# Decoder trunk: seven products in feed-forward blocks 3 and 5 too, quarter sums on GpSimd, and recorded draws for the order search

## The chip, the cores and the metric

The kernel runs on one core of one Trainium2 chip. The metric is the device time of one launch in microseconds (us); before the change it is 2908.55 us, the median of three runs (2907.97 to 2912.36). The engines are named as in the profile: PE is TensorE (matmul), DVE is VectorE, ACT is ScalarE, POOL is GpSimd, SP issues the DMAs.

## The reference, cut to what matters

The program is a decoder trunk of four layers over 512 tokens of 1024 features in float32. Each layer is a token mixer (sparse attention, mLSTM, RWKV-7, sparse attention again) followed by a gated feed-forward with a causal convolution of width 3, each after an RMSNorm and with a residual add. The change touches the feed-forward:

```
def conv_ffn(h, w_up, conv_w, conv_b, w_down):
    gate, val = jnp.split(h @ w_up, 2, axis=-1)
    gate = causal_dwconv(gate, conv_w, conv_b)
    return (jax.nn.silu(gate) * val) @ w_down
...
for i in range(DEPTH):
    h = rmsnorm(x, norm_mixer[i])
    x = x + mixer(h)
    h = rmsnorm(x, norm_ffn[i])
    x = x + conv_ffn(h, ffn_w_up[i], ffn_conv_w[i], ffn_conv_b[i], ffn_w_down[i])
return rmsnorm(x, final_norm)
```

The inner width is 2816, which is 22 blocks of 128 channels for the gate and 22 for the value.

## The kernel before, in words

**Layout.** The residual x is held feature-major, eight tiles of 128 features by 512 tokens. Every float32 product is made of three fp32r matmuls: each operand is split into a rounded part (hi, written by ACT) and the rest (lo, a subtraction on DVE, `split` at L741 and L742, and `weights` at L469 and L470), and hi·hi, lo·hi and hi·lo are summed in PSUM.

**A feed-forward stage** (`ffn`) goes over 22 blocks b. A block is made in one of two ways.

- *Plain* (`up`, `fm_block`, `mm3`): two outputs, gate and value, of 8 chunks with 3 matmuls of 512 columns each, 48 matmuls (L475 to L477). DVE makes two low weight parts of 128x1024 (L470) and the gate's scaling by R (L615).
- *Seven products* (`seven`): gate and value rows of the weight and the two halves of the contraction make a 2x2 arrangement, and so do contraction halves and token halves of the input. Seven products of 4 chunks with 3 matmuls of 256 columns give all four quarters of the result: 84 matmuls (L624). For it DVE makes four sums of weight quarters (`add`, L644), the low parts of seven weight tiles (`ring`, L742, tile slo) and seven combinations of PSUM results of 128x256 (L658 to L673).

Both end in the gate's two convolution steps on DVE (L593, L595), the product of value and gate (L602) and its split (alo). In the kernel before, SEVEN names blocks 2, 4 and 6 to 21, so that blocks 0, 1, 3 and 5 are plain.

**The input's combinations.** The seven products read four combined inputs besides plain quarters of x. `combos` makes them once in each stage: ACT scales the eight tiles of x (L549, tile tmp), then for each of four pairs four subtractions or additions of 128x256 (L558 to L561) give two tiles, and each is split into bhi (ACT) and blo (DVE, L742). The 16 operations of 128x256 stand on DVE.

**The norm beside it.** At a stage's start PE sums the squares by eight small matmuls with ones (L518, after the last of seven running sums on POOL, L509), DVE turns them into the reciprocal root rc by twelve small operations (L525, then `rsqrt`, L448 to L453), PE transposes rc (L534) and ACT copies it out as R. These transposes stand in PE's order among the matmuls of the first blocks, so what follows them on PE waits for rc.

**Down products.** `down_part` makes the partial output products of blocks 0 to 5 (from block 6 on) and of 6 to 13, one of eight outputs after each block; the rest comes at the end. They need the activations of those blocks.

**What sets the order.** The program is traced once, and class `Order` then chooses each engine's instruction order by list scheduling with durations of its own (`cost`, `LATENCY`). POOL and DVE are separate engines in it and nothing ties a POOL operation to a DVE operation beyond data. `best` searches: for each of eight phases (four mixers, four feed-forwards) 24 starting priorities with random spreads, ten rounds of `turns` each, the best few joined to what comes before, and at the end 13 perturbed passes over the whole program. Engines then run their instructions strictly in the chosen order.

Of the kernel before, what the change touches and what calls it, by code (L numbers as in the profile page):

```python
# [16 lines left out]
OP = mybir.AluOpType  # L17
# [3 lines left out]
T = 512  # L21
# [3 lines left out]
FB = 22  # L25
EPS = 1e-6

SEVEN = (2, 4) + tuple(range(6, FB))
PARTS = [6, 14]


# [16 lines left out]
TABLE = {"Silu": 1, "Sigmoid": 2, "Gelu_apprx_tanh": 3, "Exp": 0, "Tanh": 0}  # L48
SWITCH = 1283
AVOID = 500  # L50
SPREADS = (0, 50, 50, 50, 200, 200, 200, 500, 500, 500, 1000, 1000, 1000)
TICK, WARM = 10240 / 3, 3060.0
BESIDE = 22

# [1 line left out]
class Order:  # L56
# [290 lines left out]
                prio = [-(s + d) for s, d in zip(late, self.dur)]  # L347
        return best

    def best(self, tries=24, rounds=10, keep=4, log=None):  # L350

        rng = random.Random(1)
        prio, at = [], 0.0
        for a, b in zip(self.phases, self.phases[1:] + [len(self.ins)]):
            p, whole = self.part(a, b), self.part(0, b)
            found = []
            for i in range(tries):
                spread = (0, 300, 1000, 3000)[min(i, 1 + i % 3)]
                found.append(p.turns([100.0 * k + rng.gauss(0, spread) for k in range(b - a)], rounds, at))
            found.sort(key=lambda f: f[0])  # L360
            joined = []
            for T, start in found:
                t, end = whole.run(prio + [at + s for s in start])
                joined.append((end, t))
                if len(joined) == keep and max(joined)[0] - min(joined)[0] < 8000:
                    break
            end, start = min(joined, key=lambda f: f[0])
            if log:
                log(f"phase {a}-{b}: best {found[0][0]/1e3:.1f} mean {sum(f[0] for f in found)/len(found)/1e3:.1f} joined", *["%.1f" % ((e - at) / 1e3) for e, _ in joined])
            prio, at = start, end  # L370
        found = [(at, prio)] + [self.turns([s + rng.gauss(0, spread) for s in prio], 2) for spread in SPREADS]
        if log:
            log("whole:", *["%.1f" % (T / 1e3) for T, _ in found])
        return min(found, key=lambda f: f[0])

    def apply(self, tc, start):
        info = mybir.DependencyInfo(mybir.DependencyClass.NoSync, mybir.DependencyReason.DATA)
# [8 lines left out]
class Core:  # L386
# [153 lines left out]
    def combos(self, g, ap):  # L540


        nc, v = self.nc, self.nc.vector
        H = T // 2
        hx = {}

        def scaled(i):
            hx[i] = self.tmp()
            nc.scalar.activation(hx[i], self.x[i], AF.Copy, scale=g[:, i:i + 1])  # L549
            self.spill(i, self.x[i])  # L550

        out = []
        for k, need in enumerate(((0, 4, 1), (5, 2, 3), (6,), (7,))):
            for i in need:
                scaled(i)
            a, b = hx[k], hx[k + 4]
            t, u = self.tmp(), self.tmp()
            v.tensor_tensor(t[:, :H], a[:, :H], a[:, H:], op=OP.subtract)  # L558
            v.tensor_tensor(t[:, H:], b[:, H:], t[:, :H], op=OP.add)
            v.tensor_tensor(u[:, :H], a[:, H:], b[:, H:], op=OP.subtract)  # L560
            v.tensor_tensor(u[:, H:], b[:, :H], t[:, H:], op=OP.subtract)  # L561
            for w in (t, u):
                hi = self.xp.tile([128, T], F32R, name="bhi", tag="x", bufs=DC)
                lo = ap.tile([128, T], F32R, name="blo", tag="blo", bufs=DC)
                self.split(hi, lo, w)
                out.append((hi, lo))
        return out

    def ffn(self, ly, gcur, gnext, nsplit=True):
        nc, tc, A = self.nc, self.tc, self.A  # L570
        H = T // 2
        with ExitStack() as es:
# [132 lines left out]
            for b in range(FB):  # L705
# [5 lines left out]
                slots[b] = free.pop(0) if free else len(slots)  # L711
                block = (seven if b in SEVEN else plain_block)(b)
                next(block)
# [1474 lines left out]
```

## Time and profile before

| what | value |
|---|---|
| runs | 2907.97, 2908.55, 2912.36 us |
| the profiled execution's own time | 2905.92 us |
| its span in the profile | 2904.2 us, mean granted TensorE clock 0.982 |
| busy on PE, DVE, ACT, POOL | 96%, 81%, 56%, 28% of the span |
| four feed-forward stages | from 370, 963, 1838 and 2542 us, some 351 to 362 us each |

A row of a timeline gives start, duration, engine, source line, operation, and tiles written and read. Consecutive starts give the pitch, which on PE and DVE is below the duration, since an engine begins an instruction while the one before drains. A window row gives the busy time of each engine in a stretch, with the number of instructions in brackets.

### The profile page before, as it was taken

To read this page: it belongs to the slowest core of one execution; us is meant where nothing else is said; L and a number is where in the kernel's file an instruction comes from. 1 tells how busy PE (TensorE), PEld (TensorE's weight loads), DVE (VectorE), ACT (ScalarE), POOL (GpSimd) and SP (SyncE) were. 2 spreads that over 40 slices of the span, in tenths; PEclk is the share of its full clock that TensorE was granted. 3 is DMA by queue.
4 is the path that set the end of the run, shared out by engine and by line. 5 is a ranking of instruction groups with operands and counts; after the bars stand their busy time and mean duration, and the time that the engine had idled before them with its cause. 6 is when DMAs were issued, how large, how long until landed. Compare 5 with 4: busy or idle time off the path is not lost. (4 is left out here: it accounts for less than half of the span.)

```text
span 2904.2 us, 48935 instructions
## 1 busy us (share of the span) xinstructions
PE 2789.4 (96%) x17960; PEld 2357.7 (81%) x17960; DVE 2363.3 (81%) x4225; ACT 1622.5 (56%) x3290; POOL 820.8 (28%) x898
## 2 busy tenths in 40 slices
PE   7999999999989999998899999999998999999998
PEld 6777889998867899986666676899987877889996
DVE  8688789897697889979557874889978688699985
ACT  4677665544575555444446665655544677565543
POOL 5476300001063100013456653100004576300001
PEclk9999999999999999999989999999999999999999
DMA  4200133445213434453200012334453100233444
GB/s 163 66 29 24 66 109 112 136 137 188 87 46 110 131 104 130 135 178 111 75 35 3 9 30 73 118 104 130 140 158 139 59 30 23 79 99 125 137 129 145
DMA packets 115423, 283.30 MB, mean 98 GB/s; under 512 B 14448, under 2 KB 26224, under 8 KB 115184
## 3 DMA queue, kind: packets, MB, share of 16 engines
q1 hardware_dynamic: 115184, 280.18, 29.7%
q8 instruction: 142, 2.33, 0.3%
q14 instruction: 97, 0.79, 0.1%
HBM read 248.67 MB, written 31.46 MB: 96 GB/s over the span
## 5 line engine op out<-in xcount | busy, mean ns | idle before, releaser
L469 ACT ACTIVATE whi<-wraw 128x1024 fp32r<-128x1024 f32 (+2 forms) x344 | 272.2, 792 | 418.6 <-PE ps L477 273.8
L624 PE MATMUL ps<-h,shi 128*128 128x256 f32 x1728 | 352.1, 281 | 0.0
L470 DVE TENSOR_TENSOR wlo<-wraw,whi 128x512 fp32r<-128x512 f32 (+2 forms) x306 | 272.6, 892 | 72.2 <-ACT whi L469 70.5
L624 PE MATMUL ps<-bhi,slo 128*128 128x256 f32 x1152 | 322.3, 280 | 0.0
L624 PE MATMUL ps<-blo,shi 128*128 128x256 f32 x1152 | 322.0, 281 | 0.0
L624 PE MATMUL ps<-bhi,shi 128*128 128x256 f32 x1152 | 321.8, 281 | 0.0
L609 POOL MEMSET tmp<- 128x2 f32 x88 | 8.2, 99 | 1098.0 <-DVE tmp L602 875.3
L624 PEld LDWEIGHTS ps<-h,shi 128*128 128x128 f32 x1728 | 282.5, 188 | 6.7
L477 PE MATMUL ps<-alo,whi 128*128 128x512 f32 x704 | 278.0, 395 | 0.0
L475 PE MATMUL ps<-ahi,whi 128*128 128x512 f32 x704 | 277.6, 395 | 0.0
L476 PE MATMUL ps<-ahi,wlo 128*128 128x512 f32 x704 | 277.1, 394 | 0.0
L475 PE MATMUL ps<-h,whi 128*128 128x512 f32 x672 | 266.0, 398 | 4.0 <-ACT whi L469 1.2
L476 PE MATMUL ps<-h,wlo 128*128 128x512 f32 x672 | 264.1, 394 | 2.0 <-DVE wlo L470 1.7
L477 PE MATMUL ps<-h,whi 128*128 128x512 f32 x672 | 263.6, 394 | 0.0
L624 PE MATMUL ps<-h,slo 128*128 128x256 f32 x864 | 242.6, 281 | 0.0
L741 ACT ACTIVATE shi<-sum 128x512 fp32r<-128x512 f32 x288 | 179.6, 625 | 110.9 <-DVE sum L644 81.2
L742 DVE TENSOR_TENSOR slo<-sum,shi 128x512 fp32r<-128x512 f32 x288 | 197.9, 688 | 47.0 <-ACT shi L741 45.4
L624 PEld LDWEIGHTS ps<-bhi,slo 128*128 128x128 f32 x1152 | 217.0, 188 | 5.2
L624 PEld LDWEIGHTS ps<-bhi,shi 128*128 128x128 f32 x1152 | 216.5, 188 | 4.5
L624 PEld LDWEIGHTS ps<-blo,shi 128*128 128x128 f32 x1152 | 216.5, 188 | 1.2
L509 POOL TENSOR_TENSOR tmp<-tmp 128x512 f32<-128x512 f32 x62 | 96.6, 1557 | 352.4 <-ACT tmp L504 348.1
L1097 POOL TENSOR_SCALAR P<-P,st,GT 128x384 f32<-128x384 f32 (+3 forms) x256 | 161.8, 646 | 81.8 <-DVE st L1095 52.0
(669 smaller groups left out, 7745.9 us busy)
## 6 DMA issues: line engine op xcount, KB each, us to landing
wraw<-in_fup_dram SPq DMA_DIRECT2D x104, 512.0 KB, 3.7
fraw<-in_fup_dram SPq DMA_DIRECT2D x72, 512.0 KB, 3.5
wraw<-in_fdn_dram SPq DMA_DIRECT2D x128, 256.0 KB, 2.7
share<-xt SPq DMA_DIRECT2D x64, 256.0 KB, 2.2
xt<-share SPq DMA_DIRECT2D x64, 256.0 KB, 3.0
wraw<-in_fdn_dram SPq DMA_DIRECT2D x64, 192.0 KB, 2.6
x<-spill SPq DMA_DIRECT2D x48, 256.0 KB, 3.1
spill<-x SPq DMA_DIRECT2D x47, 256.0 KB, 2.7
```

Source lines behind the costliest of these rows:

```text
L469: nc.scalar.activation(hi[:, s], raw[:, s], AF.Copy)
L470: (nc.gpsimd if pool else nc.vector).tensor_tensor(lo[:, s], raw[:, s], hi[:, s].bitcast(F32), op=OP.subtract)
L475: t.matmul(ps, whi, xhi, start=start, stop=False)
L476: t.matmul(ps, wlo, xhi, start=False, stop=False)
L477: t.matmul(ps, whi, xlo, start=False, stop=stop)
L509: nc.gpsimd.tensor_tensor(a2, self.acc[0], sq, op=OP.add)
L609: nc.gpsimd.memset(G[:, 0:2], 0.0)
L624: nc.tensor.matmul(ps, lhs[:, s], x, start=start and k + i == 0, stop=k == 3 and i == 2, skip_group_check=True)
L741: self.nc.scalar.activation(hi, src, AF.Copy)
L742: self.nc.vector.tensor_tensor(lo, src if src2 is None else src2, hi.bitcast(F32), op=OP.subtract)
L1097: po.tensor_scalar(P[qb], P[qb], st[:, 2, qb:qb + 1], GT[:, qb, 3 * h + 1 + br:3 * h + 2 + br], op0=OP.mult, op1=OP.mult)
```

## The change

Three things change. SEVEN becomes blocks 2 to 21, so blocks 3 and 5 of each of the four stages are made by seven products too. The 16 operations of `combos` go from DVE to POOL. `best` no longer searches: it takes one recorded seed and spread for each phase and one perturbed pass at the end, which gives another order throughout the program, the mixers included.

```
-SEVEN = (2, 4) + tuple(range(6, FB))
+SEVEN = tuple(range(2, FB))
...
-SPREADS = (0, 50, 50, 50, 200, 200, 200, 500, 500, 500, 1000, 1000, 1000)
+DRAWS = ((21, 300), (13, 1000), (13, 1000), (10, 1000), (15, 300), (4, 1000), (3, 300), (11, 3000))
+LAST = (1008, 500)
...
-    def best(self, tries=24, rounds=10, keep=4, log=None):
+    def best(self):
...
-        for a, b in zip(self.phases, self.phases[1:] + [len(self.ins)]):
-            p, whole = self.part(a, b), self.part(0, b)
-            found = []
-            for i in range(tries):
-                spread = (0, 300, 1000, 3000)[min(i, 1 + i % 3)]
-                found.append(p.turns([100.0 * k + rng.gauss(0, spread) for k in range(b - a)], rounds, at))
...
-        found = [(at, prio)] + [self.turns([s + rng.gauss(0, spread) for s in prio], 2) for spread in SPREADS]
...
-        return min(found, key=lambda f: f[0])
+        for a, b, (seed, spread) in zip(self.phases, self.phases[1:] + [len(self.ins)], DRAWS):
+            rng = random.Random(seed)
+            t, start = self.part(a, b).turns([100.0 * k + rng.gauss(0, spread) for k in range(b - a)], 10, at)
+            prio, at = self.part(0, b).run(prio + [at + s for s in start])
+        if LAST is None:
+            return at, prio
+        rng = random.Random(LAST[0])
+        return self.turns([s + rng.gauss(0, LAST[1]) for s in prio], 2)
...
-            v.tensor_tensor(t[:, :H], a[:, :H], a[:, H:], op=OP.subtract)
-            v.tensor_tensor(t[:, H:], b[:, H:], t[:, :H], op=OP.add)
-            v.tensor_tensor(u[:, :H], a[:, H:], b[:, H:], op=OP.subtract)
-            v.tensor_tensor(u[:, H:], b[:, :H], t[:, H:], op=OP.subtract)
+            po.tensor_tensor(t[:, :H], a[:, :H], a[:, H:], op=OP.subtract)
+            po.tensor_tensor(t[:, H:], b[:, H:], t[:, :H], op=OP.add)
+            po.tensor_tensor(u[:, :H], a[:, H:], b[:, H:], op=OP.subtract)
+            po.tensor_tensor(u[:, H:], b[:, :H], t[:, H:], op=OP.subtract)
```

Line numbers of the changed kernel from `combos` on are 12 below those of the kernel before (L742 becomes L730).

How the order moves is shown at three places. First, DVE at the start of the first feed-forward stage, before: x, gains, h are the residual's split, ms, rq_t, rc and rq_u the norm's small tiles, tmp the combinations, blo their low parts.

```order
L497 SCALAR_TENSOR_TENSOR h_4157<-x_85,gains_88,h_4156 128x512
L644 TENSOR_TENSOR sum_4437<-fraw_4431 128x512
L558 TENSOR_TENSOR tmp_4275<-tmp_4263 128x256
L560 TENSOR_TENSOR tmp_4276<-tmp_4263,tmp_4267 128x256
L559 TENSOR_TENSOR tmp_4275<-tmp_4267,tmp_4275 128x256
L525 TENSOR_SCALAR ms_4240<-ps_4235 128x4
L561 TENSOR_TENSOR tmp_4276<-tmp_4267,tmp_4275 128x256
L448 TENSOR_SCALAR rq_t_4243<-ms_4240 128x4
L558 TENSOR_TENSOR tmp_4301<-tmp_4271 128x256
L449 TENSOR_SCALAR rc_4242<-rq_t_4243 128x4
L560 TENSOR_TENSOR tmp_4302<-tmp_4271,tmp_4289 128x256
L451 TENSOR_TENSOR rq_u_4244<-rc_4242 128x4
```

The same place now, on DVE:

```order
L485 SCALAR_TENSOR_TENSOR h_4157<-x_85,gains_88,h_4156 128x512
L513 TENSOR_SCALAR ms_4240<-ps_4235 128x4
L436 TENSOR_SCALAR rq_t_4243<-ms_4240 128x4
L437 TENSOR_SCALAR rc_4242<-rq_t_4243 128x4
L439 TENSOR_TENSOR rq_u_4244<-rc_4242 128x4
L440 SCALAR_TENSOR_TENSOR rq_u_4244<-rq_u_4244,ms_4240 128x4
L441 SCALAR_TENSOR_TENSOR rc_4242<-rq_u_4244,rc_4242 128x4
```

Two more rounds like the last three rows follow, then a wlo and four blo. The norm's twelve small operations, which alternated with the combinations (tmp), now follow each other, and the low parts blo come behind them.

Second, POOL at the same place now; L497 (L509 before) is the last running sum of squares, which PE's L506 (L518 before) waits for.

```order
L497 TENSOR_TENSOR tmp_4162<-tmp_4122,tmp_4160 128x512
L546 TENSOR_TENSOR tmp_4275<-tmp_4263 128x256
L548 TENSOR_TENSOR tmp_4276<-tmp_4263,tmp_4267 128x256
L547 TENSOR_TENSOR tmp_4275<-tmp_4267,tmp_4275 128x256
L546 TENSOR_TENSOR tmp_4301<-tmp_4271 128x256
L549 TENSOR_TENSOR tmp_4276<-tmp_4267,tmp_4275 128x256
L547 TENSOR_TENSOR tmp_4301<-tmp_4289,tmp_4301 128x256
L548 TENSOR_TENSOR tmp_4302<-tmp_4271,tmp_4289 128x256
L549 TENSOR_TENSOR tmp_4302<-tmp_4289,tmp_4301 128x256
```

The first eight combinations are shown, and the other eight follow them: all 16 stand directly behind the last running sum, where POOL had only two-column memsets (L609) until the stage's end before.

Third, DVE where block 3's first work stood before, among that of block 2: wlo_4590 is the first low weight part of block 3, L615 the gate's scaling of block 1, the slo are block 2's, alo0 is block 0's result.

```order
L602 TENSOR_TENSOR tmp_4424<-ps_4204,tmp_4422 128x512
L470 TENSOR_TENSOR wlo_4590<-wraw_4588,whi_4589 128x1024
L658 TENSOR_TENSOR tmp_4475<-ps_4435,tmp_4457 128x256
L742 TENSOR_TENSOR slo_4536<-sum_4528,shi_4535 128x512
L615 TENSOR_TENSOR tmp_4511<-ps_4351,R_4261 128x512
L742 TENSOR_TENSOR alo0_4427<-tmp_4424,ahi0_4426 128x512
L742 TENSOR_TENSOR slo_4553<-sum_4530,shi_4552 128x512
```

And now, where block 3's sums and first low parts stand:

```order
L632 TENSOR_TENSOR sum_4594<-fraw_4588 128x512
L730 TENSOR_TENSOR alo1_4525<-tmp_4522,ahi1_4524 128x512
L632 TENSOR_TENSOR sum_4612<-sum_4594,wraw_4587 128x512
L632 TENSOR_TENSOR sum_4682<-wraw_4587,fraw_4588 128x512
L661 TENSOR_TENSOR tmp_4534<-ps_4435,tmp_4457 128x256
L730 TENSOR_TENSOR slo_4617<-sum_4612,shi_4616 128x512
L730 TENSOR_TENSOR slo_4635<-wraw_4587,shi_4634 128x512
L730 TENSOR_TENSOR slo_4653<-sum_4594,shi_4652 128x512
L632 TENSOR_TENSOR sum_4684<-wraw_4587,sum_4612 128x512
```

The two weight subtractions of a plain block (wlo) have gone, and eleven operations of 128x512 stand in their place, of which seven are in these rows (four sum, three slo).

## Rows read from the trace of the kernel before

**Rows 1.** The page: the span, the busy time of PE and DVE (part 1) and the shares of the chain that ended last (part 4).

```profile
span 2904.2 us, 48935 instructions
...
PE 2789.4 (96%) x17960; PEld 2357.7 (81%) x17960; DVE 2363.3 (81%) x4225; ACT 1622.5 (56%) x3290; POOL 820.8 (28%) x898
...
PE 18%; DVE 4%; issue 1%; ACT 1%; POOL 0%; DVEq 0%; ACTq 0%; POOLq 0%
```

**Rows 2.** Windows over whole stages: the first and the third feed-forward.

```profile
370.00:722.00 352.00, 349.52 (x2249) 316.43 (x2247) 309.20 (x553) 180.51 (x310) 14.69 (x34) 1.00 0.42 133
...
1838.00:2189.00 351.00, 349.50 (x2256) 317.42 (x2257) 309.65 (x554) 181.80 (x311) 16.64 (x32) 1.00 0.42 132
```

**Rows 3.** The timeline of PE in plain block 0 of the first stage: two matmuls of 512 columns, with 23 more between them.

```profile
374.37 0.39 PE L475 MATMUL ps<-h,whi 128*128 128x512 f32 x1
...
379.81 0.39 PE L475 MATMUL ps<-h,whi 128*128 128x512 f32 x1
```

**Rows 4.** The chain that ended last, in order of time: a run of matmuls of 256 columns of the seven products, start, length and count.

```profile
2781.72 7.43 PE ps L624 x63
```

**Rows 5.** Windows of 20 us over the first blocks of the first stage (columns: length; PE, PEld, DVE, ACT, POOL busy; clock).

```profile
371.00:391.00 20.00, 19.66 (x93) 16.10 (x92) 20.00 (x48) 15.93 (x26) 1.23 (x4) 1.00 0.24 79
391.00:411.00 20.00, 20.00 (x130) 18.18 (x129) 18.63 (x31) 11.36 (x18) 0.13 (x2) 1.00 0.32 106
411.00:431.00 20.00, 20.00 (x130) 18.21 (x129) 17.91 (x32) 10.31 (x17) 0.13 (x2) 1.00 0.27 90
```

**Rows 6.** The timeline of DVE in the same stretch: pairs of rows that follow each other directly.

```profile
382.09 0.43 DVE L558 TENSOR_TENSOR tmp<-tmp 128x256 f32<-128x256 f32 x1
382.43 0.43 DVE L560 TENSOR_TENSOR tmp<-tmp 128x256 f32<-128x256 f32 x1
...
384.03 1.23 DVE L470 TENSOR_TENSOR wlo<-wraw,whi 128x1024 fp32r<-128x1024 f32 x1
385.17 1.30 DVE L742 TENSOR_TENSOR blo<-tmp,bhi 128x512 fp32r<-128x512 f32 x2
...
388.18 0.76 DVE L593 SCALAR_TENSOR_TENSOR tmp<-tmp,cw 128x512 f32<-128x512 f32 x1
388.84 0.70 DVE L644 TENSOR_TENSOR sum<-wraw,fraw 128x512 f32<-128x512 f32 x1
...
390.10 0.70 DVE L742 TENSOR_TENSOR slo<-sum,shi 128x512 fp32r<-128x512 f32 x1
390.70 0.70 DVE L742 TENSOR_TENSOR slo<-wraw,shi 128x512 fp32r<-128x512 f32 x1
```

**Rows 7.** The norm's marks in the first stage: PE's eight small matmuls, and DVE's first small operation behind them.

```profile
371.99 1.05 PE L518 MATMUL ps<-ones,tmp 128*128 128x1 f32 x8 [0.34 <-POOL tmp L509]
...
374.01 0.15 DVE L525 TENSOR_SCALAR ms<-ps 128x4 f32<-128x4 f32 x1
```

**Rows 8.** By line: POOL's two-input operation of 128x256 in the RWKV mixer (count; shortest, median, longest in ns).

```profile
L1806 POOL TENSOR_TENSOR h<-h,rlv x35: 659/673/1115, 1530.1 to 1744.8; 128x256 f32<-128x256 f32 x35
```

**Rows 9.** The timelines of POOL and then of DVE in one stretch of the RWKV mixer, where a chain of reciprocal-root operations (L451 to L453, here 128x64) meets two-input operations on POOL.

```profile
1433.20 2.80 POOL L470 TENSOR_TENSOR wlo<-wraw,whi 128x1024 fp32r<-128x1024 f32 x1
1435.96 4.18 POOL L1551 TENSOR_TENSOR h<-tmp,h 128x512 fp32r<-128x512 f32 x3
...
1430.26 0.22 DVE L452 SCALAR_TENSOR_TENSOR tmp<-tmp 128x64 f32<-128x64 f32 x1
...
1433.71 2.37 DVE L452 SCALAR_TENSOR_TENSOR tmp<-tmp 128x64 f32<-128x64 f32 x1
1436.00 0.68 DVE L1567 COPY rk<-ps 128x512 f32<-128x512 f32 x1
1436.60 0.73 DVE L453 SCALAR_TENSOR_TENSOR tmp<-tmp 128x64 f32<-128x64 f32 x1
1437.25 1.77 DVE L742 TENSOR_TENSOR hid<-tmp,hid 128x512 fp32r<-128x512 f32 x1
1438.94 1.28 DVE L451 TENSOR_TENSOR tmp<-tmp 128x64 f32<-128x64 f32 x1
```

**Rows 10.** By line on DVE (shortest, median, longest in ns): the residual's split beside POOL's running sums, one small operation of the norm's width in the RWKV mixer, and one at the feed-forward norms.

```profile
L497 DVE SCALAR_TENSOR_TENSOR h<-x,gains,h x64: 737/1352/2380, 6.0 to 2544.6; 128x512 fp32r<-128x512 f32 x64
...
L449 DVE TENSOR_SCALAR gst<-rq_t x8: 161/172/652, 1607.8 to 1809.4; 128x8 int32<-128x8 int32 x8
...
L451 DVE TENSOR_TENSOR rq_u<-rc x27: 151/161/165, 29.0 to 2893.4; 128x4 f32<-128x4 f32 x27
```

**Rows 11.** The timeline of PE after two waits at the end of the first feed-forward.

```profile
717.17 0.50 PE L475 MATMUL ps<-h,whi 128*128 128x512 f32 x1 [1.23 <-ACT whi L469]
718.59 0.47 PE L780 MATMUL ps<-h,mQ 128*128 128x512 f32 x1 [0.92 <-DVE mQ L742]
...
720.63 0.63 PE L780 MATMUL ps<-h,mQ 128*128 128x512 f32 x1
721.06 0.63 PE L781 MATMUL ps<-h,mQ 128*128 128x512 f32 x1
```

**Rows 12.** The norm's marks on PE around the two sparse-attention mixers: the first begins at 26.68 and ends at the mark in Rows 7, the second lies between these two.

```profile
26.68 0.95 PE L518 MATMUL v<-ones,tmp 128*128 128x1 f32 x8
...
2189.51 0.95 PE L518 MATMUL v<-ones,tmp 128*128 128x1 f32 x8
...
2543.62 1.05 PE L518 MATMUL ps<-ones,tmp 128*128 128x1 f32 x8 [0.26 <-POOL tmp L509]
```

More of the change, by code (lines that the diff above doesn't have):

```diff
@@ L348, in turns @@
         return best
-    def best(self, tries=24, rounds=10, keep=4, log=None):
-        rng = random.Random(1)
+    def best(self):
         prio, at = [], 0.0
-        for a, b in zip(self.phases, self.phases[1:] + [len(self.ins)]):
-            p, whole = self.part(a, b), self.part(0, b)
-            found = []
-            for i in range(tries):
-                spread = (0, 300, 1000, 3000)[min(i, 1 + i % 3)]
-                found.append(p.turns([100.0 * k + rng.gauss(0, spread) for k in range(b - a)], rounds, at))
[L360 to L370, printed above, removed]
-        found = [(at, prio)] + [self.turns([s + rng.gauss(0, spread) for s in prio], 2) for spread in SPREADS]
-        if log:
-            log("whole:", *["%.1f" % (T / 1e3) for T, _ in found])
-        return min(found, key=lambda f: f[0])
+        for a, b, (seed, spread) in zip(self.phases, self.phases[1:] + [len(self.ins)], DRAWS):
[6 more added lines that the diff above has]
+        return self.turns([s + rng.gauss(0, LAST[1]) for s in prio], 2)
     def apply(self, tc, start):
@@ L540, in combos @@
     def combos(self, g, ap):
-        nc, v = self.nc, self.nc.vector
+        nc, po = self.nc, self.nc.gpsimd
         H = T // 2
```

## The prediction

> **What bounds the kernel now.** I read the page first: PE is busy 96% of the span and holds by far the largest share of the chain that ended last, DVE comes next with 81% [rows 1]. The windows over whole stages show that the feed-forwards are tighter than that: PE is busy 349.5 of 351 to 352 us there, DVE 309 to 310 [rows 2]. So a matmul saved in a feed-forward is saved from the time, as long as DVE keeps up. Then the windows over a stage's first 60 us: DVE is busy 20.00 of 20, then 18.63, then 17.91, while PE has no idle time after the start [rows 5]. The reader is to see that DVE is full just where the change gives it more work, and that this place is the start of a stage, before any down product, which costs DVE little, can stretch PE's side.
>
> **The change part by part.** All sums are made against the profiled execution's own 2905.92 us; it lies 2.6 us below the median of 2908.55, which I add at the end. About 0.2% (6 us) is what a measurement of this kernel can tell from no change.
>
> *Blocks 3 and 5 by seven products: PE.* 24 pitches of 512 columns take 5.44 us, 0.2267 each [rows 3]; 63 matmuls of 256 columns take 7.43 us, 0.1179 each [rows 4]. A plain block is 48 x 0.2267 = 10.88 us, a seven-product block 84 x 0.1179 = 9.90. That is 0.98 us saved a block, and with two blocks in each of four stages 7.8 us.
>
> By the Trainium skill (TensorE: Matmul & The Clock Gate, Back-to-back issue gap) a warm matmul alone is followed after N/2.4 plus 2.5 ns. By that, as an estimate, the two blocks' kinds would be 10.36 and 9.18 us, the saving 9.5 us, and my sum 1.7 us lower; the trace's pitches are 5 to 8% longer than that, so the measurement decides.
>
> *The same blocks: DVE.* From consecutive starts [rows 6] an operation of 128x512 takes 0.60 us, one of 128x256 0.34, a three-operand one 0.66, a 128x1024 one 1.14. A plain block is 2 x 1.14 + 0.60 + 2 x 0.66 + 2 x 0.60 = 5.4 us of DVE beside 10.9 of PE. A seven-product block is 11 x 0.60 (four sums, seven low parts) + 7 x 0.34 + 2 x 0.66 + 2 x 0.60 = 11.5 beside 9.9. Blocks 3 and 5 were the cover: DVE caught up under them by 5.5 us each. Now four seven-product blocks follow each other before down products can come, and DVE loses 1.6 us on PE in each. Moving the combinations takes 16 x 0.34 = 5.4 us from DVE.
>
> *DVE against PE in the new order, if POOL cost DVE nothing.* I count from the norm's mark T to the second low part of block 5, the place where the sums come out worst. DVE has 55 operations of 128x512, 8 three-operand ones, 21 of 128x256, 2 of 128x1024 and 12 small ones of 0.16 [rows 10]: 33.0 + 5.3 + 7.1 + 2.3 + 1.9 = 49.6 us. Its first small operation started 2.0 us after the mark [rows 7], so it is done at T + 51.6. PE has 78 matmuls of 512 and 266 of 256 columns before it needs that tile, with 1.3 for the norm's own: 17.7 + 31.4 + 1.3 = T + 50.4. In the other three stages (83 and 265; 78 and 266, with one 128x256 less on DVE; 81 and 266) PE arrives at T + 51.4, 50.4 and 51.0. So PE waits 1.3, 0.3, 0.9 and 0.6 us, 3.1 in all. This is parity: any further delay of DVE in these 50 us is PE's delay, and nothing later gives it back, since PE is full to the end of a stage [rows 2].
>
> *The combinations on POOL.* A two-input operation of 128x256 takes POOL 0.67 us [rows 8], twice DVE's 0.34. The 16 of them stand in one row directly behind the last running sum, so they begin at T and hold POOL for at least 10.8 us. The trace shows what that does to DVE. Beside POOL's two-input operations a reciprocal-root step of 0.22 us took 2.37, and the next ones 0.73 and 1.28, each ending when POOL's operation ended, one DVE operation for each POOL operation [rows 9]; only the copy from PSUM between them, with no SBUF input, was not held. The residual's split takes 0.74 alone and 1.35 in the median, mostly beside POOL's sums; small operations of 0.17 took up to 0.65, a POOL operation's length [rows 10, 8]. So DVE operations whose inputs are in SBUF and POOL's two-input operations take turns.
>
> In the new order exactly such operations meet the row on POOL: eleven of the norm's twelve small ones, then the weights' and the combinations' low parts. Three of the 16 on POOL fit into the 2.0 us before the norm's first operation, when DVE had little to do. The other 13 each hold DVE once: 13 x 0.67 = 8.7 us a stage. The bounds are 0, if turns could be taken in gaps that DVE has anyway, and 16 x 0.67 = 10.8. I take 8.7, near the upper end, because DVE had no gaps there [rows 5] and the chained small operations in rows 9 were held one for one. What is queued behind them: rc first. The eleventh held step ends at T + 2.0 + 11 x (0.67 + 0.16) = T + 11.1, but PE, with 30 matmuls of 512 columns in between, stands at rc's transposes at T + 7.7 and waits. Behind rc stand R, every gate scaling, and the first low parts of block 2.
>
> The Trainium skill (SBUF — State Buffer, SBUF: two separate sides) states a rule against this change: a port pair is shared by GpSimd and VectorE and is held exclusively for a whole instruction, not split, against a VectorE operation with two SBUF inputs or in a two-port mode. By that rule, as an estimate, all 16 would hold DVE, 10.8 us a stage instead of 8.7, and my sum would be 8 us higher. Rows 9 agree in kind; how many of the 16 find DVE waiting, no row of before shows.
>
> *Sum.* DVE's lateness is 3.1 + 4 x 8.7 = 37.9 us, and PE waits for it. 2905.9 - 7.8 + 37.9 = 2936.0; plus 2.6 for the median, 2938.7.
>
> *The other edits.* ACT gets six more operations for each converted block; it was busy 10 to 16 of 20 us [rows 5] and I cost this at nothing; if that cover is gone, low parts come later still and the sum rises. The block's weights are loaded with the same bytes. The gates' memsets on POOL now stand behind the combinations until about T + 16, before they are needed. The new draws move every phase. One row of size: the same sparse-attention mixer took 345.3 us between its marks in one place and 354.1 in the other [rows 7, 12], under two orders and with different neighbours. I take 0 for the draws, since nothing in the trace says which order is better, and keep 9 us either way.
>
> **The rivals.** *The gain lands.* Mechanism: the combinations on POOL fill gaps, because POOL waits for ACT's scaled tiles and DVE slips through. Place: the first 12 us of each stage. Price: 2905.9 - 7.8 + 0 to 3.1, plus 2.6, 2901 to 2904; it is faster from the point where DVE's total lateness in a stage stays under 7.8 / 4 = 1.9 us, that is, where fewer than two of the 16 hold DVE. For it: DVE did have 1.4 and 2.1 us of idle time in the second and third window [rows 5], and two of the scaled tiles are made late. Against it: rows 9, and that the new order fills these gaps with 12 us of work.
>
> *Half of it.* The low parts that wait for ACT's high parts would have waited anyway, so that half of the 8.7 us hides there: 2938.7 - 17.4 = 2921.
>
> *More than that.* PE's wait for rc lets its clock fall. After two waits of 1.23 and 0.92 us matmuls of 512 columns came 0.43 us apart, the 1.2 GHz level, instead of 0.23 [rows 11]. If each stage lost another 3.5 us, the time would be 2953. Against it: PE stands waiting for DVE in this stretch, so slow matmuls are mostly hidden.
>
> *The draws decide.* A new order in the mixers that is better or worse by 9 us or more. It shifts any of the cases; alone with a landed gain it would give 2893 to 2912.
>
> **How the numbers follow.** Forecast (DVE held, 2925 to 2948 with the draws): 0.58. Half: 0.16. Gain landed: 0.14. More: 0.08. Draws by far more than 9 us: 0.04. The predicted time is 2939. The range reaches down to 2907, which takes in the half case with good draws and leaves out the landed gain, and up to 2953. Faster by over 0.2% (below 2902.7) is most of the landed gain and the good side of the draws: 0.15. Within 0.2% is the rest of it and the edge of the half case: 0.10. Slower: 0.75.
>
> **What would show it.** Right: at each stage's start the small operations of the norm take about 0.7 us instead of 0.16 beside POOL's row; PE's wait for rc's transposes shows as idle time of some 3 to 7 us; PE waits further in blocks 2 to 5 for low parts (slo) from DVE, 8 to 11 us a stage in all; the seven-product pitch stays 0.118; from block 10 on PE is full as before. Wrong: if the small operations stay at 0.16, there are no turns, and the stage shortens by 2 us. If they are held but PE is not, then DVE's 49.6 us of work is not the bound I take it for. If the mixers differ by more than the feed-forwards, the draws decided.

## The result and the profile after

The changed kernel takes 2936.46 us, the median of four runs (2933.39 to 2939.44); the kernel before, in the same comparison, 2910.45 us (2907.97 to 2914.26). The ratio is 1.0095, with a 95% interval of 1.0082 to 1.0108: slower by about 26 us. The forecast was 2939, in a range of 2907 to 2953.

The page of the changed kernel, to be set against [rows 1]: the span, the busy time of PE and DVE, and the page's own shares of the chain.

```profile
span 2931.6 us, 49698 instructions
...
PE 2789.4 (95%) x18248; PEld 2360.3 (81%) x18248; DVE 2416.9 (82%) x4281; ACT 1638.7 (56%) x3338; POOL 885.0 (30%) x962
```

PE is busy for the same time as before, the span is 27.4 us longer: PE has more idle time. DVE is busy 54 us longer, with 56 operations more: 64 were taken from it and 120 came. The next view says where. These are windows from one norm's mark to the next: the four feed-forwards, then the RWKV mixer, the third of the four mixers (columns as in [rows 5]).

```profile
375.26:733.01 357.75, 348.83 (x2309) 317.43 (x2309) 322.72 (x566) 182.94 (x319) 28.55 (x49) 1.00 0.42 131
976.49:1339.63 363.14, 353.72 (x2328) 320.96 (x2326) 323.08 (x567) 183.63 (x318) 31.25 (x56) 0.99 0.42 130
1852.50:2213.37 360.87, 353.18 (x2329) 320.93 (x2330) 324.53 (x570) 186.54 (x323) 33.16 (x48) 1.00 0.41 129
2564.36:2916.21 351.85, 345.15 (x2301) 314.50 (x2301) 310.88 (x553) 181.99 (x314) 25.19 (x44) 1.00 0.39 123
...
1339.63:1852.50 512.87, 477.09 (x4135) 350.31 (x4135) 364.90 (x717) 280.73 (x737) 275.24 (x274) 0.98 0.16 51
```

The same windows of the kernel before:

```profile
371.99:721.91 349.92, 347.77 (x2239) 315.31 (x2240) 307.21 (x552) 178.52 (x307) 12.82 (x33) 1.00 0.42 133
964.21:1315.93 351.72, 350.42 (x2256) 317.41 (x2256) 309.66 (x553) 177.65 (x306) 15.62 (x40) 1.00 0.42 135
1839.50:2189.51 350.01, 350.01 (x2258) 317.80 (x2259) 308.89 (x553) 180.81 (x309) 15.75 (x32) 1.00 0.42 132
2543.62:2887.87 344.25, 343.42 (x2228) 311.76 (x2228) 296.54 (x540) 177.34 (x302) 9.82 (x28) 1.00 0.39 126
...
1315.93:1839.50 523.57, 486.53 (x4134) 359.68 (x4134) 367.71 (x719) 284.04 (x738) 276.32 (x273) 0.94 0.15 50
```

Before, the feed-forwards so took 344 to 352 us from mark to mark, not the 351 to 362 of the table ahead. They became 7.8, 11.4, 10.9 and 7.6 us longer, 37.7 in sum, the four mixers 9.2 us shorter, and the ends 1.0 us shorter: 27.5 in all. A feed-forward in which PE had idled for 0 to 2 us now has 7 to 9 us of it. The equal busy time of PE on the page is the sum of two moves that cancel: 9.3 us more in the four feed-forwards, 9.4 less in the RWKV mixer, whose clock was 0.98 and not 0.94.

Now the first twelve us of the first feed-forward. DVE's timeline is cut to the small operations of the norm and the first low parts; under it stands POOL's row of combinations.

```profile
376.82 0.15 DVE L513 TENSOR_SCALAR ms<-ps 128x4 f32<-128x4 f32 x1
377.00 0.52 DVE L436 TENSOR_SCALAR rq_t<-ms 128x4 int32<-128x4 int32 x1
377.55 0.66 DVE L437 TENSOR_SCALAR rc<-rq_t 128x4 int32<-128x4 int32 x1
378.25 0.67 DVE L439 TENSOR_TENSOR rq_u<-rc 128x4 f32<-128x4 f32 x1
...
381.74 0.16 DVE L441 SCALAR_TENSOR_TENSOR rc<-rq_u,rc 128x4 f32<-128x4 f32 x1
...
382.77 0.16 DVE L441 SCALAR_TENSOR_TENSOR rc<-rq_u,rc 128x4 f32<-128x4 f32 x1
...
384.00 3.59 DVE L730 TENSOR_TENSOR blo<-tmp,bhi 128x512 fp32r<-128x512 f32 x4
```

```profile
377.45 0.73 POOL L547 TENSOR_TENSOR tmp<-tmp 128x256 f32<-128x256 f32 x1
378.15 0.75 POOL L546 TENSOR_TENSOR tmp<-tmp 128x256 f32<-128x256 f32 x1
...
388.14 1.19 POOL L549 TENSOR_TENSOR tmp<-tmp 128x256 f32<-128x256 f32 x1
```

An operation on 4 columns takes 0.67 us beside POOL's row and 0.16 where the row pauses for an input (381.74, 382.77); before it took 0.15 to 0.165 always [rows 10]. Starts on the two engines alternate 0.70 us apart. Behind the norm the same goes on with long operations: four blo take 3.59 us where a pair took 1.30 [rows 6], and POOL's operation takes 1.19 instead of 0.67 [rows 8]. Against the median of the same operation alone, DVE's operations beside POOL's in the first 20 us behind the mark are longer by 7.9, 8.2, 7.8 and 7.6 us, 31.5 in all, with 15 or 16 of them held a stage.

PE's waits, by what released them: in the first stage from 384 to 445 us, and in the third just behind its mark (sum, times, longest).

```profile
PE ps L612 <- DVE slo L730: 2.3, 1, 2.3
PE ps L612 <- ACT shi L729: 2.3, 3, 1.1
PE ps L612 <- ACT tmp L643: 0.9, 1, 0.9
PE ps L464 <- DVE wlo L458: 0.8, 2, 0.6
```

```profile
PE ps L522 <- DVE rc L441: 3.8, 1, 3.8
```

The norm's transposes (L522) wait in the third stage for 3.8 us and in the fourth for 2.0; in the second for 0.5, with 2.5 us for wlo close behind; in the first rc was in time. The rows of waits leave out two things. One is a slow start after a wait, here of matmuls of 256 columns that otherwise follow at 0.12 us:

```profile
396.30 0.38 PE L612 MATMUL ps<-h,slo 128*128 128x256 f32 x1 [2.34 <-DVE slo L730]
396.53 0.41 PE L612 MATMUL ps<-h,shi 128*128 128x256 f32 x2
```

The other is the clock. It fell behind two of these waits. Windows over a stretch of the second stage, from within the wait for wlo on, and one of the third, right behind the wait for rc:

```profile
988.70:995.50 6.80, 6.10 (x14) 4.78 (x15) 6.80 (x8) 3.31 (x6) 4.05 (x4) 0.50 0.51 154
1865.87:1869.25 3.38, 3.38 (x12) 2.70 (x11) 3.38 (x4) 2.38 (x4) 3.38 (x4) 0.51 0.54 155
```

The granted clock is 0.50 there, the 1.2 GHz level, and matmuls of 512 columns follow at 0.43 us. In the first 120 us of the first and the fourth stage it stays at 1.00. So I measure **PE's lost time**: over all rows of PE's timeline in the first 120 us behind the mark, the time by which starts lie further apart than 0.228 us for 512 columns and 0.118 for 256 (plus 0.015 for jitter). It is 0.9, 1.0, 0.9 and 1.8 us before, 4.6 in sum, and 10.9, 12.6, 12.6 and 9.9 after, 46.0 in sum, of which some 4 us are slow matmuls in the two stretches above. In the rest of the four stages, to the next mark, it is 6.0 before and 10.0 after.

### The profile page after: what moved, and what is told of

Same layout as the page of the kernel before. It is cut to its first block, busy times and chain, and to the rows that moved or that the text cites. A ratio compares the mean times of both kernels' runs of the same rounds, so it can differ in the third digit from the quotient of the medians.

```text
span 2931.6 us, 49698 instructions
## 1 busy us (share of the span) xinstructions
PE 2789.4 (95%) x18248; PEld 2360.3 (81%) x18248; DVE 2416.9 (82%) x4281; ACT 1638.7 (56%) x3338; POOL 885.0 (30%) x962
## 5 line engine op out<-in xcount | busy, mean ns | idle before, releaser
L457 ACT ACTIVATE whi<-wraw 128x512 fp32r<-128x512 f32 (+2 forms) x328 | 255.4, 779 | 379.7 <-PE ps L465 210.1
L612 PE MATMUL ps<-h,shi 128*128 128x256 f32 x1920 | 401.5, 282 | 4.5 <-DVE tmp L652 2.5
L612 PE MATMUL ps<-bhi,shi 128*128 128x256 f32 x1280 | 353.6, 282 | 7.6 <-ACT shi L729 7.5
L612 PE MATMUL ps<-bhi,slo 128*128 128x256 f32 x1280 | 356.5, 282 | 0.9 <-DVE slo L730 0.8
L612 PE MATMUL ps<-blo,shi 128*128 128x256 f32 x1280 | 354.1, 281 | 0.0
L612 PEld LDWEIGHTS ps<-h,shi 128*128 128x128 f32 x1920 | 318.0, 189 | 17.4 <-ACT shi L729 4.2
L612 PE MATMUL ps<-h,slo 128*128 128x256 f32 x960 | 269.2, 281 | 2.5 <-DVE slo L730 2.5
L612 PEld LDWEIGHTS ps<-bhi,shi 128*128 128x128 f32 x1280 | 238.8, 188 | 16.5 <-ACT shi L729 10.7
L730 DVE TENSOR_TENSOR slo<-sum,shi 128x512 fp32r<-128x512 f32 x320 | 218.8, 684 | 22.4 <-ACT shi L729 21.1
L464 PE MATMUL ps<-h,wlo 128*128 128x512 f32 x544 | 216.0, 402 | 6.3 <-DVE wlo L458 5.5
L463 PE MATMUL ps<-h,whi 128*128 128x512 f32 x544 | 214.5, 401 | 7.0 <-DVE tmp L724 1.8
L465 PE MATMUL ps<-h,whi 128*128 128x512 f32 x544 | 212.9, 399 | 1.0 <-DVE h L485 1.0
L497 POOL TENSOR_TENSOR tmp<-tmp 128x512 f32<-128x512 f32 x62 | 97.0, 1564 | 360.9 <-ACT tmp L492 338.9
L1085 POOL TENSOR_SCALAR P<-P,st,GT 128x128 f32<-128x128 f32 (+3 forms) x256 | 163.5, 653 | 84.5 <-DVE st L1083 39.8
```

The lines of the kernel that those rows point to most:

```text
L457: nc.scalar.activation(hi[:, s], raw[:, s], AF.Copy)
L463: t.matmul(ps, whi, xhi, start=start, stop=False)
L464: t.matmul(ps, wlo, xhi, start=False, stop=False)
L465: t.matmul(ps, whi, xlo, start=False, stop=stop)
L497: nc.gpsimd.tensor_tensor(a2, self.acc[0], sq, op=OP.add)
L612: nc.tensor.matmul(ps, lhs[:, s], x, start=start and k + i == 0, stop=k == 3 and i == 2, skip_group_check=True)
```

## Experiments

In several runs the order was kept: the changed kernel's program was traced and planned as it stands, and each instruction of the edited program got the planned start of its twin (PLAN[0] is set while that order is planned). The diffs show the lines that matter. Sums by stage come from one profiled execution of each kernel.

**The combinations back on DVE, order kept** (comb_dve).

```diff
-        nc, po = self.nc, self.nc.gpsimd
+        nc, po = self.nc, self.nc.gpsimd if PLAN[0] else self.nc.vector
```

> The changed kernel with the 16 combinations of a stage back on DVE, every engine's order as in the changed kernel (the combinations stand in DVE's order where POOL had begun them in the plan). Theory (POOL's row holds DVE in turns and PE waits for DVE): the 31.5 us by which DVE's operations were held beside the row go, and 64 x 0.34 = 21.8 us of work come to DVE, so 9.7 us less than the changed kernel: about 2927 us; the norm's small operations are back at 0.16 us. Rival (the row costs DVE nothing, PE waits only because blocks 3 and 5 no longer let DVE catch up): 21.8 us more, about 2958. Second rival (the new order is what costs): no change, 2936.

Measured: 2920.98 us (ratio to before 1.0040, 1.0027 to 1.0053). The feed-forwards take 1417.6 us in sum, 16.0 less than in the changed kernel, PE's lost time is 31.1 us, and the norm's small operations are back at 0.15 to 0.17 us. The direction is the theory's and the rivals fall. But DVE got 21.8 us of work for 31.5 us of turns, and the gain is larger than that difference: the two do not reach PE in full, and the next run shows by how much.

**POOL fills instead of computing, order kept** (comb_memset).

```diff
-            po.tensor_tensor(t[:, :H], a[:, :H], a[:, H:], op=OP.subtract)
...
+            else:
+                for w in (t[:, :H], t[:, H:], u[:, :H], u[:, H:]):
+                    po.memset(w, 0.0)
```

> The changed kernel in its own order, but POOL fills the 16 half tiles of a stage with zeros instead of computing the combinations (the combinations of the input's quarters are left out): the row on POOL has no inputs, DVE's work and PE's are unchanged. Theory: no turns, the 31.5 us of held DVE time go, and 45.5 - 31.5 = 14 us of PE's waits stay: about 2905 us. Rival (blocks 3 and 5 as cover are the whole cause): 2936, as the changed kernel. If filling also holds DVE, in between, and the small operations show it.

Measured: 2917.78 us (1.0035, 1.0010 to 1.0060); the profiled execution, the fastest of ten, 2909.50. That is 13 us above the theory's 2905 and 18 below the rival's 2936. Its feed-forwards take 1409.8 us, 23.8 less than in the changed kernel, and PE's lost time is 25.3. The timeline of DVE behind the norm's mark, and under it POOL's fills in the same stretch:

```profile
376.45 0.16 DVE L513 TENSOR_SCALAR ms<-ps 128x4 f32<-128x4 f32 x1 [0.16 <-PE ps L506]
376.65 0.22 DVE L436 TENSOR_SCALAR rq_t<-ms 128x4 int32<-128x4 int32 x1
376.91 0.24 DVE L437 TENSOR_SCALAR rc<-rq_t 128x4 int32<-128x4 int32 x1
377.18 0.16 DVE L439 TENSOR_TENSOR rq_u<-rc 128x4 f32<-128x4 f32 x1
377.38 0.16 DVE L440 SCALAR_TENSOR_TENSOR rq_u<-rq_u,ms 128x4 f32<-128x4 f32 x1
...
378.76 0.16 DVE L441 SCALAR_TENSOR_TENSOR rc<-rq_u,rc 128x4 f32<-128x4 f32 x1
379.04 1.23 DVE L458 TENSOR_TENSOR wlo<-wraw,whi 128x1024 fp32r<-128x1024 f32 x1
380.18 2.49 DVE L734 TENSOR_TENSOR blo<-tmp,bhi 128x512 fp32r<-128x512 f32 x4
383.94 0.69 DVE L636 TENSOR_TENSOR sum<-sum,wraw 128x512 f32<-128x512 f32 x1 [1.27 <-DMA wraw<-in_fup_dram]
```

```profile
375.02 2.88 POOL L553 MEMSET tmp<- 128x256 f32 x11
380.93 1.33 POOL L553 MEMSET tmp<- 128x256 f32 x5 [3.02 <-DVE blo L734]
```

Eleven fills run until 377.90, beside the first of the norm's small operations. From L439 on these keep their 0.16 us; only the two with one input before them (L436, L437) take 0.22 and 0.24, where the kernel before had 0.15 to 0.17. Five more fills run beside the four blo, which take 2.49 and not 3.59. So it is the two-input operations that cost, not POOL's being busy (one-input operations on POOL were not tried). Two things are also seen. DVE now idles for 1.27 us on a load of weights, a gap that turns had filled in the changed kernel: that is one reason why of 31.5 us of turns only 20.7 (46.0 - 25.3) reach PE. Some 3 of these 20.7 are the clock: it falls once in this run's first 120 us of the stages, for 3.4 us, against 6.8 and 3.4 in the changed kernel. And without any turn, and without the combinations' work anywhere, PE still loses 25.3 us, 20.7 more than before. The theory had 14. The two losses lie in different places: in the first 32 us behind the marks the changed kernel loses some 25 us and this run 5, and from there to 120 us both lose some 20.

**Blocks 3 and 5 plain, the combinations on POOL** (plain_pool).

```diff
-SEVEN = tuple(range(2, FB))
+SEVEN = (2, 4) + tuple(range(6, FB))
```

> Blocks 3 and 5 plain as in the kernel before, the combinations on POOL, the order drawn by the recorded seeds. Theory: DVE is held 7.9 us a stage and relieved of 5.4, so it stands 2.5 us later than before until block 3, and blocks 3 and 5 give it 5.5 us each to catch up; PE waits at the norm and in block 2 for 2.5 us a stage, 10 in all, and the drawn mixers give some 9 back: about 2910 us. Rival (what holds DVE is passed to PE whole, 7.9 us a stage): 2910 + 31.5 - 9 = 2932. Rival (POOL's row costs nothing): about 2901.

**The recorded seeds alone** (draws_alone): the same line, and the combinations on DVE.

```diff
-SEVEN = tuple(range(2, FB))
+SEVEN = (2, 4) + tuple(range(6, FB))
...
-        nc, po = self.nc, self.nc.gpsimd
+        nc, po = self.nc, self.nc.vector
```

> The kernel before with nothing but the recorded seeds in place of the search: blocks 3 and 5 plain, the combinations on DVE. Theory (the changed kernel's mixers are 9.2 us shorter because their order was drawn anew): the feed-forwards stay at 350 us, the mixers lose some 9 us: about 2901 us, the RWKV mixer some 10 us shorter. Rival (the mixers are shorter because of what runs ahead of them): 2910, mixers as before.

Measured: 2959.46 us (1.0176, 1.0161 to 1.0192) and 2925.23 us (1.0063, 1.0044 to 1.0083). Both totals miss, because of the mixers: the RWKV mixer took 549.4 and 524.9 us, and with the seeds alone the four mixers took 1472.3 us in sum, not less than the 1465.3 before. So the theory of draws_alone fell: the changed kernel's shorter mixers do not come with the seeds. The feed-forwards answer the question that they were made for. With comb_dve and the changed kernel they fill a table (sum of the four feed-forwards, and PE's lost time in brackets, us):

| | combinations on DVE | on POOL | filled with zeros |
|---|---|---|---|
| blocks 3 and 5 plain | 1399.4 (6.9) | 1415.1 (21.0) | |
| by seven products | 1417.6 (31.1) | 1433.6 (46.0) | 1409.8 (25.3) |

The seeds do little to the feed-forwards (1395.9 and 4.6 before). POOL's row costs 15.6 us, the seven products 18.1, and both together 34.2: they add up. With plain blocks the theory had 10 for POOL's row and the rival 31.5; the measured 15.6 are nearer to the theory.

**The row stretched** (row_longer).

```diff
+            for _ in range(4 if not PLAN[0] else 0):
+                po.tensor_tensor(scr, self.ident, self.ones, op=OP.add)
```

> The changed kernel in its own order with four more two-input additions of 128x128 on POOL behind every four combinations, 16 a stage, from two constant tiles into a tile that nobody reads. Theory (each two-input operation on POOL holds DVE once, and PE waits for DVE here): at some 0.4 us each, estimated from 0.67 us for twice the columns, 6.4 us of held DVE time a stage, of which 70 to 100% reaches PE: 18 to 26 us more than the changed kernel, about 2958. Rival (the turns of the row are over where DVE has time to give): 2936 to 2940.

Measured: 2962.04 us (1.0208, 1.0156 to 1.0261), the feed-forwards 22.8 us longer. The number is the forecast one, the mechanism is not: DVE was held for only 26.7 us in all. Two rows of its timeline show what took the place:

```profile
393.65 1.23 DVE L734 TENSOR_TENSOR blo<-tmp,bhi 128x512 fp32r<-128x512 f32 x1 [3.12 <-ACT bhi L733]
...
398.50 1.22 DVE L734 TENSOR_TENSOR blo<-tmp,bhi 128x512 fp32r<-128x512 f32 x1 [2.22 <-ACT bhi L733]
```

DVE stands still for bhi, which ACT makes from a combination that POOL made late. So this run tells nothing of turns; the two at the end were made for that.

**The mixers' order with the feed-forwards of before** (mix_order, five_dve): the recorded seeds plan the feed-forwards, the changed kernel's planned starts lead in the mixers. five_dve also has block 5 by seven products.

```diff
+            if i % 2 == 0:
...
+                start = [theirs[c + k] - base for k in range(b - a)]
```

> The kernel before in what it computes where (blocks 3 and 5 plain, the combinations on DVE), with the changed kernel's planned order in the four mixers and the recorded seeds in the feed-forwards. Theory (the mixers' 9.2 us come from the order that they were drawn in, and the feed-forwards' 37.7 from the two edits alone): mixers of 1456 us in sum, feed-forwards of 1399, about 2900 us. Rival (the mixers were short because of what ran beside them): 2925, as with the seeds alone.

> As the run with mixed orders, with block 5 by seven products and block 3 plain, the combinations on DVE. Theory (a plain block lets DVE catch up by more than 5 us, and what PE waits for comes from four seven-product blocks in a row): 3.9 us of matmuls saved, 0 to 2 us of waits a stage come: feed-forwards of 1395 to 1403 us in sum, 2896 to 2904. Rival (each seven-product block ahead of the down products costs its 2 us of DVE's lateness at once): feed-forwards of some 1408 us.

Measured: 2926.44 us (1.0059, 1.0036 to 1.0083) and 2926.52 us (1.0080, 1.0049 to 1.0111). The first misses: the order was not really carried (RWKV mixer 522.1 us), and behind the third feed-forward's mark PE lost some 9 us at the seam. The feed-forwards, 1416.3 and 1416.8 us, are those of the second run's rival (some 1408) and not its theory (1395 to 1403), but with such seams the two runs do not tell what block 5 costs.

**Another last draw** (other_draw): one seed of the changed kernel.

```diff
-LAST = (1008, 500)
+LAST = (1009, 500)
```

> The changed kernel with another seed in the last draw of the order (1009 for 1008). Theory (the mixers' times, the RWKV mixer's above all, hang on the draw, and the feed-forwards' do not): feed-forwards of 1434 us within 6, the RWKV mixer anywhere between the 513 us of the changed kernel and the 549 seen with other draws, 2936 to 2972 in all. Rival (draws are worth nothing on the chip): 2936 within 4.

Measured: 2967.89 us (1.0198, 1.0179 to 1.0218). The feed-forwards take 1438.0 us, 4.4 from the changed kernel's; the mixers 1484.6, 28.6 longer, of which the RWKV mixer 16.0, as the theory had it. A draw is worth more than the whole change.

**The mixers' order held** (kept_mixers, kept_five): as mix_order, with every engine's order inside a mixer tied.

```diff
+                    for j, k in zip(row, row[1:]):
+                        self.follow[k].add(j)
+                        self.after[j].add(k)
```

> As the run with mixed orders, but every engine's order inside a mixer is held to that of the changed kernel, and the whole is planned in four turns at the end. Theory (an order that is really carried over carries its time): mixers of 1456 to 1460 us in sum, the RWKV mixer 513 to 516; feed-forwards with blocks 3 and 5 plain and the combinations on DVE 1396 to 1404; about 2900 us, faster than the kernel before by 0.3%. Rival (what a draw gave in one program is lost at the seams with other feed-forwards): the feed-forwards stay at the 1416 of the run with mixed orders, about 2915.

> As the run with kept mixers, with block 5 by seven products and block 3 plain, the combinations on DVE. Theory (with one plain block among blocks 2 to 5 DVE is late by at most 1 us a stage at block 5): the feed-forwards 0 to 4 us shorter in sum than in the run with kept mixers. Rival (each seven-product block this early costs PE 2 us of waits a stage): 4 us longer.

Measured: 2907.79 us (1.0009, 0.9993 to 1.0025; twelve runs from 2901.15 to 2923.57) and 2915.47 us (1.0024, 1.0006 to 1.0041; 2907.26 to 2934.59). The profile of the first is the theory's, with mixers of 1458.5 and feed-forwards of 1398.5 us; the median is no better than before. The profiles of the two say why. Windows over the RWKV mixer, whose own instructions stand in the same order on PE, DVE, ACT and POOL in both; kept_mixers, then kept_five:

```profile
1323.33:1836.02 512.69, 476.47 (x4132) 349.81 (x4133) 363.96 (x718) 280.68 (x737) 274.81 (x273) 0.98 0.16 51
```

```profile
1328.13:1864.25 536.12, 501.22 (x4133) 367.85 (x4131) 365.14 (x713) 281.69 (x737) 274.41 (x273) 0.93 0.15 47
```

23.4 us apart, with the same busy time on DVE, ACT and POOL, and a granted clock of 0.98 and 0.93 of 2.4 GHz in the mean. PE's matmuls and weight loads alone were slower. Over the twelve runs of kept_mixers the time follows the clock too: 2901 us at 0.987, 2924 at 0.978. Block 5 by seven products: kept_five's feed-forwards take 1407.8 us, 9.4 more, as the rival would have it, with 6.5 of that in the second one, whose clock was 0.99 there and 1.00 in kept_mixers. The clock is not the whole of it. At a mean clock of 0.987 kept_mixers took 2901.15 us and kept_five 2908.74 and 2910.61, and a straight line of time against clock, fitted to the 24 runs with one slope, puts kept_five 6.6 us higher (standard error 0.8). That is the rival's direction (4 us longer), not the theory's. Whether the block itself costs this or the order that was drawn around it is not shown.

**The same 16 additions elsewhere** (turns_later, turns_slack): nothing waits for them, and nothing that they write is read.

```diff
+            full[k:k + 16] = [gates[3] + 0.001] * 16
```

In turns_slack gates[14] stands for gates[3].

> The changed kernel in its own order with 16 more two-input additions of 128x128 on POOL in each stage, of two constants into a tile that nobody reads, put behind the combinations and the first gates' memsets, some 32 us behind the norm's mark, where POOL has 12 us with nothing to do and nobody waits for what they write. In the run with the longer row such an addition took some 0.5 us and DVE's operations were hardly held more in sum (26.7 us of 31.5), since DVE waited there for combinations that came late. Theory (POOL's two-input operations hold DVE wherever they meet, and DVE sets PE's pace up to block 5): 16 x 0.53 = 8.5 us of held DVE time a stage, 6 to 8.5 of it reach PE, 24 to 34 us more than the changed kernel, about 2965. Rival (what costs is that the row makes the norm's chain and the combinations late, not the turns): within 5 us of 2936.

> The same 16 additions, behind the fifteenth memset of the gates, in the middle of the stage, where DVE is busy 18 of 20 us and PE 20. Theory (only where DVE sets the pace does a held DVE operation cost): DVE is held the same 8.5 us a stage, its lead there takes most of it: 0 to 2 us a stage, 2936 to 2944. Rival (DVE has no lead in the middle of a stage either): about 2965, as with the additions early.

Measured: 2952.19 us (1.0143, 1.0124 to 1.0162) and 2945.10 us (1.0130, 1.0111 to 1.0149). DVE beside the additions of turns_later:

```profile
411.91 0.89 DVE L636 TENSOR_TENSOR sum<-fraw 128x512 f32<-128x512 f32 x1
412.73 0.94 DVE L734 TENSOR_TENSOR alo<-tmp,ahi 128x512 fp32r<-128x512 f32 x1
...
415.33 0.41 DVE L665 TENSOR_TENSOR tmp<-ps,tmp 128x256 f32<-128x256 f32 x1
415.66 0.67 DVE L734 TENSOR_TENSOR slo<-sum,shi 128x512 fp32r<-128x512 f32 x1
```

```profile
410.54 13.12 POOL L557 TENSOR_TENSOR scr<-ident,ones 128x128 f32<-128x128 f32 x16
```

An operation of 0.68 us takes 0.94: turns again, but short ones, and the operation with one input in PSUM (415.33) keeps its 0.41. In sum DVE is held 10.4 us in turns_later and 11.0 in turns_slack, a third of what was expected. An addition takes POOL 0.46 us at the least and 0.79 in the median here, but it holds DVE for 0.16 to 0.17 in the mean, not for its whole length. The feed-forwards are 9.6 us longer with the additions early, 93% of what DVE lost, and 4.2 us longer with them in the middle, 38%. So in the feed-forwards the rivals of both runs fall; the early share is the theory's (70 to 100%), the later 4.2 us lie in its 0 to 8, and what was wrong in both is the size of a turn. The early 93% are not waits alone. From 32 us behind the marks on PE's lost time grows by some 10 us, and 6 of that are slow matmuls: in each stage the granted clock falls to 0.50 for 3.4 us behind the additions, where in the changed kernel it stayed at 1.00. The rest of the totals is in the mixers, which the edit does not touch.

## Why the prediction was right

The time, the sign and the mechanism came as forecast. The two sizes under it did not; they erred to opposite sides, and the mixers covered what was left.

- **PE's saving.** Right. The pitches stayed (256 columns at 0.118 us in both kernels), and the account closes with the forecast 7.8 us, to about 1 us, which the allowance for jitter leaves open: 41.4 us of lost time more behind the marks (46.0 - 4.6), 4.0 more in the rest of the stages (10.0 - 6.0), less 7.8, is 37.6; the feed-forwards grew by 37.7.
- **DVE's turns with POOL.** Shown, by comb_memset above all. The term was 13 x 0.67 = 8.7 us a stage. Nearly all 16 held DVE, not 13, but at 0.49 us each (31.5 / 64): a small operation ends with POOL's after 0.67 us, and 0.16 of that is its own. That makes 7.9 a stage, close to the term. What was wrong is that all of it would reach PE: 20.7 of 31.5 did, some 3 of them by way of the clock. The lower bound's reason, gaps that DVE has anyway, held for a third; the 1.27 us wait for weights is one of them, and the profile before could not show it, since DVE was full there.
- **DVE against PE without turns.** The term that was mis-sized most. It said PE waits for 3.1 us in all; comb_memset shows 18.4 more than with plain blocks (25.3 - 6.9). I had block 5's second low part done at T + 51.6 in the first stage. Two rows give it: comb_memset's, 55.6 us behind its mark of 375.13 when it ends, and the changed kernel's, 60.8 behind 375.26.

```profile
430.06 0.69 DVE L734 TENSOR_TENSOR slo<-sum,shi 128x512 fp32r<-128x512 f32 x1
```

```profile
435.40 0.69 DVE L730 TENSOR_TENSOR slo<-sum,shi 128x512 fp32r<-128x512 f32 x1
```

The count of operations was right, 98. Their sum was 52.2 us and not 49.6, since an operation of 128x512 comes 0.63 us after the one before in the mean of this stretch, not 0.60, and one of 128x256 after 0.37, not 0.34; and DVE idled for 2.1 us, for which the sum had nothing, though [rows 5] had shown 1.4 and 2.1 us of idle time in this place before the change. (DVE's first small operation came earlier than counted, 1.3 us behind the mark and not 2.0.) Pairs that follow each other directly [rows 6] are among the fastest. At parity with PE, 5% of 50 us is 10 us over the four stages.

- **The sum.** Turns and parity were forecast at 34.8 + 3.1 = 37.9 us; measured they are 20.7 + 18.4 = 39.1. That this was right is luck: the two errors cancelled. The feed-forwards still grew by 37.7 and not by the forecast 30.1 (37.9 - 7.8), since 2.3 us of lost time came with the seeds (6.9 - 4.6) and 4.0 in the rest of the stages; and the mixers, put at 0, gave 9.2 back. That the total lies within 3 us is luck a second time; the sign is not.
- **Where PE waits.** Partly as forecast: 3.8 and 2.0 us at the norm's transposes in two stages, not in all. In blocks 2 to 5 PE waits more for ACT's shi, 7.6 us in the four stages, than for DVE's slo, 3.3. ACT was busy for 4.4 to 7.4 of each 10 us there in the first stage, and waited for DVE's sums for some 23 us in the four: for the most part it is the same delay one step on, though ACT also waited for buffers that PE was still reading, and no run separates the two.
- **The rivals.** The landed gain fell. The half fell as a time, but its mechanism, waits that hide a held operation, took a third of the turns. The rival of the falling clock came true in part: behind PE's waits for wlo and rc the clock fell in two of the four stages, for 10.2 us in all, with some 4 us of lost time, where the rival had 3.5 us in each stage. The draws, taken as 0 with 9 us either way, gave 9.2 us back, just outside; other_draw and plain_pool show that 9 was too narrow for them.
- **Left open.** How much of the RWKV mixer's 10.7 us is its order and how much the clock of that execution (0.94 and 0.98). With its order kept it took 513 to 517 us in six of seven other executions and 536 in one.

## What to carry to other kernels

Before an operation goes to POOL, look at what DVE runs beside it: POOL's two-input operations take turns with DVE's operations on SBUF, and a chain of tiny ones, such as a norm's, then pays a full POOL operation for each. When two engines are at parity, add the idle time and take the mean pitch over a whole stretch, not the fastest pair. And compare stage by stage from mark to mark: here a search seed moved the total by more than the edit, and a total alone would have told nothing of either.

## What the runs showed of the hardware

- POOL's fills (no input) held no two-input DVE operation and lengthened two one-input ones from 0.16 to 0.22 and 0.24 us in the first stage. Its two-input operations held DVE's operations on SBUF, each by 0.49 us in the mean with 128x256 and by 0.16 with 128x128 (10.4 us / 64), and were lengthened themselves: 128x256 from 0.67 to 1.19.
- The granted clock fell to 0.50, the 1.2 GHz level, during a wait of PE of 2.5 us in the second stage and right behind one of 3.8 us in the third.
- The clock granted to PE differs between executions of one kernel (kept_mixers: 2901 us at 0.987, 2924 at 0.978). With the same order inside the RWKV mixer it took 512.7 us at 0.98 in one kernel and 536.1 at 0.93 in another, and 549.4 at 0.90 under another order (plain_pool):

```profile
1331.16:1880.52 549.36, 508.64 (x4133) 373.49 (x4133) 361.74 (x720) 283.34 (x740) 274.26 (x274) 0.90 0.15 48
```
